# Hybrid decoder step on one core: rows of the norms' factors by transposing spread columns

## The chip, the cores and the metric

The kernel runs on one core of a Trainium2 chip. The metric is device time in microseconds, the median of several executions. TensorE appears in the profile as PE (matmuls) and PEld (its weight loads), VectorE as DVE, ScalarE as ACT, GpSimd as POOL, and the queue that issues the transfers as SP.

## What is computed

The reference is one inference step of one layer, for a prompt of 1024 tokens and for 8 sequences of 4 new tokens, 1056 tokens of width 1024 in all. Each sub-layer stands between two RMS norms:

```python
def rmsnorm(x, g):
    xf = x.astype(jnp.float32)
    y = xf * lax.rsqrt(jnp.mean(xf * xf, axis=-1, keepdims=True) + RMS_EPS)
    return (y * g.astype(jnp.float32)).astype(x.dtype)
...
    def half_ffn(x, j, gpre, gpost):
        y = swiglu(rmsnorm(x, g[gpre]), ffn_w_gate[l, j], ffn_w_up[l, j], ffn_w_down[l, j])
        return x + 0.5 * rmsnorm(y, g[gpost])

    x = half_ffn(x, 0, 0, 1)
    h = rmsnorm(x, g[2])
    ...
    u = jnp.concatenate([u_m, u_a], axis=-1)
    x = x + rmsnorm(u @ w_out[l], g[3])
    x = half_ffn(x, 1, 4, 5)
```

Between the two feed-forward halves, `h` is projected and passes through four mLSTM heads and eight heads of sliding-window attention. What matters here is the factor of a norm, `rsqrt(mean(x*x) + eps)`: one number per token.

## The kernel before

Activations are kept transposed: the 1024 features on partitions, in eight blocks of 128, and the tokens along the free axis. The 1056 tokens are cut into four quarters `q` of `QW` = 264 columns: 256 prompt tokens and 8 of the new ones. Two quarters form a half `g`.

There are three phases: the first feed-forward half, the mixer with `w_out`, the second feed-forward half. In each, products with weights (`pl`, `gu`, `pd`, `pz`, `pv`, `po`, `pw`) run over blocks of 128 outputs and all quarters. Each product is made of three matmuls in a reduced f32 format: weights and activations are split into a high and a low part by `split` (a cast on ACT, a subtraction on DVE), and `mm3` and its inlined copies multiply high by high, high by low and low by high. Weights come in through two buffers named `raw`.

A norm's factor is made as follows. The squares of the features are summed into a tile `acc`. `col_stats` sums over partitions by products with a column of ones and gives a PSUM tile `cs` with three columns: column `j` has, on its 128 partitions, the sums of the tokens that begin at `WIN[j]`, with `WIN = [0, 128, 136]`; so the third column repeats tokens 136 to 255 and adds the last eight. `rstd` turns them into factors by some ten small DVE operations on 128x3 elements. `row_bcast` makes a row of them again, 264 wide and repeated on all 128 partitions, in a PSUM tile `rb`: column `j` is read with its one element repeated 128 times along the free axis, as the stationary operand of a product with the identity. Two products are 128 columns wide, the third takes the last eight columns of the identity only. ACT then copies `rb` to SBUF, as `cr` in `post` (L443) or as `rrow` in `set_row` (L283). The tiles `cs`, `rb` and some others share a single PSUM buffer (tag `c`), so each is used only after the one ahead of it has been read.

`post` ends a sub-layer for one quarter: statistics, `row_bcast`, then y times `cr` plus the residual for four pairs of blocks (L448, L449) with the squares for the next norm, its statistics, and a second `row_bcast` into `rrow`. It runs for all four quarters of phases 1 and 2 with both rows, and for quarters 0 to 2 of phase 3 with `cr` alone: 11 calls of the first kind, 8 of the second. The last quarter of phase 3 is done by the class `Last`, in token layout with transposes, and makes no row. At the start, `load_x` loads tokens, computes the factors in token layout and makes the row of a quarter by two products with the identity and one with the eight new tokens' factors `xtr`.

The order of the work is written by a small planner, `Order`. Its clock `now` advances by a booked price with every product that `pe` issues: 4 x max(n, 64) / 2400 us for a plain f32 product of n columns, about 0.11 for a product of the reduced format and 0.11 for a transpose. After each group of three matmuls `tick` runs the side tasks (`load_x`, `post`, `blocks` and others) that have come due; each yields the time after which its next step is due, counted from the clock ahead of the step.

Of the kernel before, what the change touches and what calls it, by code (L numbers as in the profile page):

```python
# [16 lines left out]
P = 128  # L17
# [8 lines left out]


WIN = [0, 128, 136]
ROWP = [(0, 128, 0), (128, 128, 0), (256, 8, 120)]
STEPS = {1: [(0, 1), (2, 3)], 2: [(0, 1), (2, 3)], 3: [(0, 1), (2,), (3,)]}  # L30
NSLOT, NW, NRAW, NTMP = 66, 8, 2, 8
BANKS = dict(mm=3, a=2, b=2, c=1)
# [115 lines left out]
def pe(K, out, lhsT, rhs, start=True, stop=True, tr=False, **kw):  # L148
    n = int(np.prod(rhs.shape[1:]))
    if tr:  # L150
        K.nc.tensor.transpose(out, lhsT, rhs)  # L151
        K.od.now += 0.11
        return
    K.nc.tensor.matmul(out, lhsT, rhs, start=start, stop=stop, **kw)  # L154
    if rhs.dtype == F32R:
        K.od.now += 0.0025 + (n if n >= 213 else 256) / 2400
    else:
        K.od.now += (4 if rhs.dtype == F32 else 1) * max(n, 64) / 2400
# [7 lines left out]
def slot(K, name, dt=F32):  # L166
    return K.sp.tile([P, 2 * QW], dt, tag="s", name=nm(K, name))


def pair(t):  # L170
    return t.rearrange("p (a t) -> p a t", a=2)
# [10 lines left out]
def bank(K, name, tag="mm"):  # L182
    return K.pp[tag].tile([P, 512], F32, tag=tag, name=nm(K, name))


def sbank(K, name):
    return bank(K, name, "c")
# [64 lines left out]
def row_bcast(K, col):  # L252

    ps = sbank(K, "rb")
    for j, (a, w, b) in enumerate(ROWP):
        pe(K, ps[:, a:a + w], col[:, j:j + 1].to_broadcast([P, P]), K.ident[:, b:b + w])
    return ps[:, 0:QW]


# [20 lines left out]
def set_row(K, q, ps):  # L280

    row = K.cp.tile([P, QW], F32, tag=f"rrow{q}", name=nm(K, "rrow"), bufs=1)
    K.nc.scalar.copy(row, ps)  # L283
    K.r[q] = row


def stash(K, q, kp, x):

    t = K.dp.tile([P, 2 * QW], F32, tag=f"xs{q}{kp}", name=nm(K, "xs"))
    K.nc.sync.dma_start(t, x)  # L290
    K.xs[q][kp] = t


def load_tokens(K, src, w):

    t = [slot(K, "xt")[0:w, 0:512] for _ in range(2)]
    for i in range(2):
        K.nc.sync.dma_start(t[i], src[:, i * 512:(i + 1) * 512])
    return t


def token_norm(K, tt, both=False):

    nc = K.nc
    n = len(tt)
    ss = K.kp.tile([P, 6], F32, tag="xss", name=nm(K, "xss"), bufs=2)
    nc.vector.memset(ss, 1.0)
    for j, t in enumerate(tt):
        for i in range(2):
            w = t[i].shape[0]  # L310
            jk = tmp(K, "jk", 512)[0:w]
            o = ss[0:w, n * i + j:n * i + j + 1]
            if both and i == 0:
                nc.vector.tensor_tensor_reduce(out=jk, in0=t[i], in1=t[i], scale=1.0, scalar=0.0,
                                               op0=ALU.mult, op1=ALU.add, accum_out=o)
            else:
                nc.scalar.activation(jk, t[i], AF.Square, accum_out=o)
    s = small(K, "xsn", n)
    nc.vector.tensor_tensor(s, ss[:, 0:n], ss[:, n:2 * n], op=ALU.add)
    return rstd(K, s)  # L320


def load_sample(K):

    ps = bank(K, "xsT", "a")
    for k in range(KT):
        pe(K, ps[:, 32 * k:32 * k + 32], K.xt[k // 4][:, (k % 4) * P:(k % 4) * P + P], K.ident[0:32, 0:32], tr=True)
    K.xsT = slot(K, "xsT")[:, 0:256].rearrange("p (k t) -> p k t", k=KT)
    K.nc.vector.tensor_copy(K.xsT, ps[:, 0:256].rearrange("p (k t) -> p k t", k=KT))


def load_x(K, q):

    nc = K.nc
    tt = [load_tokens(K, K.A["x_prompt"][0, (2 * q + j) * P:(2 * q + j + 1) * P], P) for j in range(2)]
    if q == 0:
        K.xt = load_tokens(K, K.A["x_sample"].rearrange("b t d -> (b t) d"), 32)
    yield XW[0]
    with K.tc.high_priority():
        r = token_norm(K, tt + [K.xt] if q == 0 else tt, q == 0)  # L340
        if q == 0:
            K.xtr = K.cp.tile([32, 1], F32, tag="xtr", name="xtr")
            nc.vector.tensor_copy(K.xtr, r[0:32, 2:3])
    x = [slot(K, "xr") for _ in range(4)]
    for kp in range(4):

        ps = bank(K, "xT")
        for i in range(2):
            k = 2 * kp + i
            for j, t in enumerate(tt):  # L350
                pe(K, ps[:, (2 * i + j) * P:(2 * i + j + 1) * P], t[k // 4][:, (k % 4) * P:(k % 4) * P + P], K.ident,
                   tr=True)
        nc.scalar.copy(pair(x[kp])[:, :, 0:2 * P], ps.rearrange("p (a t) -> p a t", a=2))
        if q == 0 and kp == 0:
            load_sample(K)
        nc.gpsimd.tensor_copy(pair(x[kp])[:, :, 2 * P:QW], K.xsT[:, 2 * kp:2 * kp + 2, 8 * q:8 * q + 8])
        yield XW[1]
    while q and ("b", 0, q - 1, 3) not in K.od.done:
        yield 0.2
    with K.tc.high_priority():  # L360
        ps = sbank(K, "rb")
        for j in range(2):
            pe(K, ps[:, j * P:(j + 1) * P], r[:, j:j + 1].to_broadcast([P, P]), K.ident)
        pe(K, ps[:, 2 * P:QW], K.xtr.to_broadcast([32, P]), K.ident[0:32, 8 * q:8 * q + 8])
        set_row(K, q, ps[:, 0:QW])
    for kp in range(4):
        stash(K, q, kp, x[kp])
    yield XW[2]
    yield from blocks(K, 0, q, x, 0)
# [8 lines left out]
def blocks(K, phase, q, x, gpre):  # L378

    K.b[q], K.X[q] = [], []  # L380
    for kp in range(4):
        b = slot(K, "xb")
        for k in (2 * kp, 2 * kp + 1):
            s = slice((k % 2) * QW, (k % 2) * QW + QW)
            K.nc.vector.scalar_tensor_tensor(b[:, s], x[kp][:, s], K.gain[:, gpre * 8 + k:gpre * 8 + k + 1], K.r[q],
                                             op0=ALU.mult, op1=ALU.mult)
        K.b[q].append(b)
        K.X[q].append(xsplit(K, b))
        K.od.done.add(("b", phase, q, kp))
        yield NP[0]  # L390
# [38 lines left out]
def post(K, phase, q, y, acc, half, nxt, gpre=None):  # L429
# [11 lines left out]
    yield PW[1]  # L441
    cr = tmp(K, "cr", QW)
    nc.scalar.copy(cr, row_bcast(K, c))  # L443
    yield 0.5
    acc = None
# [30 lines left out]
    if nxt == "mix":  # L476
        rc = K.kp.tile([P, 3], F32, tag=f"rc{q}", name=nm(K, "rc"), bufs=1)
        nc.vector.tensor_copy(rc, r)
        K.rc[q] = rc
    set_row(K, q, row_bcast(K, r))  # L480
    K.od.done.add(("r", phase, q))
    if nxt == "ffn":
# [1277 lines left out]
def program(ctx, tc, A, O):  # L1760
    K = setup(ctx, tc, A, O)
    load_gains(K)
    K.od.units += [*ffn_units(K, 0), *mix_units(K), *ffn_units(K, 1)]
    K.od.ahead = AHEAD
    K.od.spawn(load_x(K, 0))
    K.od.need(("b", 0, 0, 1))
    K.od.fill()
    for q in range(1, NQ):
        K.od.spawn(load_x(K, q), XQ[q])
    ffn(K, 1, 0, 1, "mix", 2)  # L1770
    mix(K)
    ffn(K, 3, 1, 5, None)
    K.od.drain()
# [30 lines left out]
```

## Time and profile before

| | us |
|---|---|
| median of 3 runs | 2019.58 |
| lowest, highest | 2016.46, 2020.38 |
| the profiled execution | 2019.21 |
| its span, first to last instruction | 2017.4 |

The profile is that of one execution. Matmuls are pipelined: a record's duration is its latency, and what one costs in a stream is the distance between starts. Weight loads overlap with matmuls. A row of the timeline gives the start, the time from the first start to the last end, engine, line, operation, output and inputs, the tile's shapes and the number of records; a bracket tells the idle time ahead and what ended it. A row of the windows gives a stretch, its length, each engine's busy time with its number of instructions, the granted TensorE clock, the DMA engines' share and GB/s.

### The profile page before, as it was taken

To read this page: it belongs to the slowest core of one execution; us is meant where nothing else is said; L and a number is where in the kernel's file an instruction comes from. 1 tells how busy PE (TensorE), PEld (TensorE's weight loads), DVE (VectorE), ACT (ScalarE), POOL (GpSimd) and SP (SyncE) were. 2 spreads that over 40 slices of the span, in tenths; PEclk is the share of its full clock that TensorE was granted. 3 is DMA by queue.
4 is the path that set the end of the run, shared out by engine and by line. 5 is a ranking of instruction groups with operands and counts; after the bars stand their busy time and mean duration, and the time that the engine had idled before them with its cause. 6 is when DMAs were issued, how large, how long until landed. Compare 5 with 4: busy or idle time off the path is not lost.

```text
span 2017.4 us, 40347 instructions
## 1 busy us (share of the span) xinstructions
PE 1986.5 (98%) x16178; PEld 1942.6 (96%) x16178; DVE 1168.4 (58%) x2822; ACT 874.9 (43%) x2087; POOL 35.6 (2%) x166
## 2 busy tenths in 40 slices
PE   7999999999999999999999999999999999999997
PEld 7999999999999999987999999999999999999997
DVE  5855555557238436467556758785555556534764
ACT  6533333336336332346244655353333334533553
POOL 0000000000000001100101000000000000000000
PEclk9999999999999999999999999999999999999999
DMA  6122222226346343201214143322222223545773
GB/s 234 65 85 77 90 69 74 76 95 177 108 142 208 104 102 124 68 1 38 68 53 134 57 133 116 108 78 82 65 84 80 91 64 120 167 129 162 226 223 116
DMA packets 279690, 216.66 MB, mean 107 GB/s; under 512 B 21032, under 2 KB 252640, under 8 KB 279488
## 3 DMA queue, kind: packets, MB, share of 16 engines
q1 hardware_dynamic: 279504, 214.11, 35.0%
q8 instruction: 126, 2.06, 0.5%
q14 instruction: 60, 0.49, 0.1%
HBM read 172.39 MB, written 42.49 MB: 107 GB/s over the span
## 4 chain that ended last, share of the span: by engine, by line
PE 91%; DVE 3%; DMA 3%; ACT 2%; issue 1%; SPq 0%; DVEq 0%; ACTq 0%
PE gu L154 41%; PE pd L154 23%; PE pz L154 7%; PE pw L154 4%; PE pl L154 4%; PE pv L154 3%; PE po L154 2%; DMA raw<-ffn_w_down 2%; PE cs L154 1%; PE rb L154 1%; PE swo L154 1%; PE sws L154 1%; PE E L154 1%; ACT wh L196 1%; PE swp L151 1%
## 5 line engine op out<-in xcount | busy, mean ns | idle before, releaser
L154 PE MATMUL gu<-Xh,wh 128*128 128x264 f32 x2240 | 636.6, 284 | 0.0
L154 PE MATMUL gu<-Xl,wh 128*128 128x264 f32 x2240 | 636.0, 284 | 0.0
L154 PE MATMUL gu<-Xh,wl 128*128 128x264 f32 x2240 | 635.1, 284 | 0.0
L197 DVE TENSOR_TENSOR wl<-raw,wh 128x512 fp32r<-128x512 f32 x458 | 301.6, 670 | 384.3 <-ACT wh L196 376.5
L154 PE MATMUL pd<-hq,wh 128*128 128x264 f32 x2816 | 520.8, 286 | 0.1
L196 ACT CAST wh<-raw 128x512 fp32r<-128x512 f32 x458 | 270.1, 602 | 459.4 <-PE pd L154 193.2
L154 PEld LDWEIGHTS pd<-hq,wh 128*128 128x128 f32 x2816 | 437.8, 189 | 0.4 <-ACT yo L853 0.4
L154 PEld LDWEIGHTS gu<-Xh,wh 128*128 128x128 f32 x2240 | 421.1, 188 | 0.5 <-ACT sc L752 0.2
L154 PEld LDWEIGHTS gu<-Xh,wl 128*128 128x128 f32 x2240 | 421.6, 188 | 0.0
L154 PEld LDWEIGHTS gu<-Xl,wh 128*128 128x128 f32 x2240 | 421.3, 188 | 0.0
L154 PE MATMUL pd<-hq,wl 128*128 128x264 f32 x1408 | 401.1, 285 | 0.0
L154 PEld LDWEIGHTS pd<-hq,wl 128*128 128x128 f32 x1408 | 265.4, 188 | 0.2 <-DVE wl L197 0.2
L752 ACT COPY sc<-gu 128x264 f32<-128x264 f32 x240 | 91.0, 380 | 272.2 <-PE gu L154 268.0
L197 DVE TENSOR_TENSOR wl<-ws,wh 128x512 fp32r<-128x512 f32 x160 | 108.8, 690 | 87.6 <-ACT wh L196 84.7
L763 DVE TENSOR_TENSOR h<-gu,sc 128x264 f32<-128x264 f32 x120 | 51.8, 432 | 102.2 <-PE gu L154 83.3
L154 PE MATMUL pz<-xh,wh 128*128 128x264 f32 x352 | 102.3, 291 | 0.6 <-DVE z L1684 0.6
L154 PE MATMUL pz<-xh,wl 128*128 128x264 f32 x352 | 100.8, 286 | 0.0
L154 PE MATMUL pz<-xl,wh 128*128 128x264 f32 x352 | 100.5, 285 | 0.0
L196 ACT CAST wh<-ws 128x512 fp32r<-128x512 f32 x160 | 95.9, 623 | 4.1 <-PE pl L154 2.5
L764 ACT ACTIVATE h<-h 128x264 f32<-128x264 f32 x120 | 50.9, 425 | 106.5 <-DVE h L763 106.5
L769 DVE TENSOR_TENSOR sc<-gu,sc 128x264 f32<-128x264 f32 x120 | 51.6, 432 | 56.8 <-PE gu L154 51.4
L154 PE MATMUL pl<-Xh,wh 128*128 128x264 f32 x256 | 72.9, 299 | 3.3 <-ACT Xh L196 2.1
(368 smaller groups left out, 2969.6 us busy)
## 6 DMA issues: line engine op xcount, KB each, us to landing
raw<-ffn_w_down SPq DMA_DIRECT2D x80, 512.0 KB
raw<-ffn_w_gate SPq DMA_DIRECT2D x44, 512.0 KB
raw<-ffn_w_up SPq DMA_DIRECT2D x44, 512.0 KB
h<-h SPq DMA_DIRECT2D x80, 264.0 KB
hq<-h SPq DMA_DIRECT2D x160, 132.0 KB
raw<-ffn_w_down SPq DMA_DIRECT2D x40, 384.0 KB
x<-xs SPq DMA_DIRECT2D x48, 264.0 KB
raw<-w_in SPq DMA_DIRECT2D x21, 512.0 KB
```

Source lines behind the costliest of these rows:

```text
L151: K.nc.tensor.transpose(out, lhsT, rhs)
L154: K.nc.tensor.matmul(out, lhsT, rhs, start=start, stop=stop, **kw)
L196: K.nc.scalar.copy(hi, src)
L197: (eng or K.nc.vector).tensor_tensor(lo, src, hi.bitcast(F32), op=ALU.subtract)
L752: nc.scalar.copy(sc[n][:, g], ps)
L763: nc.vector.tensor_tensor(d, bk[tg, g], sc[n][:, g], op=ALU.add)
L764: nc.scalar.activation(d, d, AF.Silu)
L769: nc.vector.tensor_tensor(sc[n][:, g], src, sc[n][:, g], op=ALU.add)
```

## The change

`row_bcast` issues three transposes, each 128 columns wide, of the spread columns in place of the three products with (parts of) the identity. The third goes to columns 136 to 263 and is issued first, then the second to 128 to 255, then the first; columns 136 to 255 are thus written twice, with the same tokens' factors. `load_x` makes its two wide parts by transposes; the part of the new tokens stays a product. The table `ROWP` goes.

```diff
 WIN = [0, 128, 136]
-ROWP = [(0, 128, 0), (128, 128, 0), (256, 8, 120)]
...
 def row_bcast(K, col):
 
     ps = sbank(K, "rb")
-    for j, (a, w, b) in enumerate(ROWP):
-        pe(K, ps[:, a:a + w], col[:, j:j + 1].to_broadcast([P, P]), K.ident[:, b:b + w])
+    for j in (2, 1, 0):
+
+        pe(K, ps[:, WIN[j]:WIN[j] + P], col[:, j:j + 1].to_broadcast([P, P]), K.ident, tr=True)
     return ps[:, 0:QW]
...
         ps = sbank(K, "rb")
         for j in range(2):
-            pe(K, ps[:, j * P:(j + 1) * P], r[:, j:j + 1].to_broadcast([P, P]), K.ident)
+            pe(K, ps[:, j * P:(j + 1) * P], r[:, j:j + 1].to_broadcast([P, P]), K.ident, tr=True)
         pe(K, ps[:, 2 * P:QW], K.xtr.to_broadcast([32, P]), K.ident[0:32, 8 * q:8 * q + 8])
```

In `pe`, `tr=True` issues `transpose(out, lhsT, rhs)` and adds 0.11 to the planner's clock.

## The prediction

> **What bounds the kernel now.** I read the head of the page first, then the chain of work that ended last by engine, then the table of windows.
>
> ```profile
> span 2017.4 us, 40347 instructions
> PE 1986.5 (98%) x16178; PEld 1942.6 (96%) x16178; DVE 1168.4 (58%) x2822; ACT 874.9 (43%) x2087; POOL 35.6 (2%) x166
> PE 91%; DVE 3%; DMA 3%; ACT 2%; issue 1%; SPq 0%; DVEq 0%; ACTq 0%
> ```
>
> PE has something in flight during 98% of the span and makes up 91% of the chain, so a microsecond of PE time that disappears from a dense stretch is normally a microsecond of the end. The exceptions are stretches where PE waits for someone else; they come below. Where the touched work lies is read from the windows of 100 us, restricted to the tile `rb`:
>
> ```profile
> core 0: us, PE busy (x) PEld busy (x) ACT busy (x), PEclk, DMA share, GB/s
> 0.00:100.00 100.00, 4.60 (x24) 3.88 (x24) 1.52 (x4) 1.00 0.44 151
> ...
> 600.00:700.00 100.00, 3.40 (x24) 3.32 (x24) 1.54 (x4) 0.98 0.53 161
> 700.00:800.00 100.00, 3.05 (x24) 2.99 (x24) 1.52 (x4) 1.00 0.42 119
> ...
> 1200.00:1300.00 100.00, 5.99 (x48) 6.00 (x48) 2.73 (x8) 0.97 0.40 131
> ...
> 1800.00:1900.00 100.00, 1.56 (x12) 1.50 (x12) 0.76 (x2) 1.00 0.59 179
> 1900.00:2000.00 100.00, 0.73 (x6) 0.75 (x6) 0.37 (x1) 1.00 0.69 208
> ```
>
> The column after the time is PE's busy time with the number of records. All 138 `rb` records are here: 24 in the start (`load_x`, four times), 114 in 19 calls of `row_bcast` of six records each (4 + 4 + 8 + 2 + 1). Nothing else is touched.
>
> **The change part by part.** First the records of one product. The groups by line, shapes kept apart:
>
> ```profile
> L154 PE MATMUL rb<-ident,r 128*128 128x128 f32 x92 | 15.4, 292 | 2.8 <-DVE v L265 1.5 <-DVE r L276 1.3
> L154 PE MATMUL rb<-ident,r 128*128 128x8 f32 x38 | 5.6, 219 | 0.0
> L151 PE MATMUL yT<-ident,y 128*128 128x128 f32 x72 | 11.1, 277 | 3.4 <-DVE y L449 1.6 <-ACT y L556 1.0 <-ACT yo L853 0.7
> ```
>
> The code asks for 19 x 2 + 4 x 2 = 46 wide products and 19 narrow ones, and the trace has 92 and 38: an f32 product is two records, each with its own weight load. The f32 transposes `yT` are 24 calls in `Last` (12 in `first`, 12 in `second`) and 3 x 16 in `store_y`, 72 in all, and 72 records: one each. So `row_bcast` goes from six records to three and `load_x` loses two of its six. The means (292, 219, 277 ns) are latencies that overlap; the price has to be read from starts. The PE timeline around the last `row_bcast`, and around three transposes in the same kind of stream:
>
> ```profile
> 1939.14 0.28 PE L154 MATMUL pd<-hq,wl 128*128 128x264 f32 x1
> ...
> 1939.51 0.28 PE L154 MATMUL pd<-hq,wl 128*128 128x264 f32 x1
> 1939.62 0.73 PE L154 MATMUL rb<-ident,r 128*128 128x128 f32 x6
> 1940.21 0.49 PE L154 MATMUL pd<-hq,wh 128*128 128x264 f32 x2
> 1940.54 0.28 PE L154 MATMUL pd<-hq,wl 128*128 128x264 f32 x1
> ```
> ```profile
> 2001.11 0.28 PE L154 MATMUL pd<-hq,wl 128*128 128x264 f32 x1
> ...
> 2001.47 0.28 PE L154 MATMUL pd<-hq,wl 128*128 128x264 f32 x1
> 2001.60 0.49 PE L151 MATMUL yT<-ident,y 128*128 128x128 f32 x3
> 2001.84 0.49 PE L154 MATMUL pd<-hq,wh 128*128 128x264 f32 x2
> 2002.17 0.28 PE L154 MATMUL pd<-hq,wl 128*128 128x264 f32 x1
> ```
>
> Three `pd` matmuls take 1939.51 - 1939.14 = 0.37 us undisturbed. With six `rb` records between them they take 1940.54 - 1939.51 = 1.03, so the six cost 0.66 us (0.11 each). Three transposes: 2002.17 - 2001.47 = 0.70, less 0.36, costs 0.34. **Saved per call: 0.32 us.** The narrow product was already as dear per record as a wide one, so that the new third transpose computes 128 columns where 8 were needed costs nothing extra.
>
> No row of before shows a transpose whose stationary operand is one column repeated. Bounds: as cheap as `yT` (0.11), or as dear as the product it replaces (0.22, its two records). The product's weight load already reads the repeated column, at the pace of its neighbours, so I take 0.11 and keep 0.22, no gain at all, as the other end.
>
> Eighteen calls stand in streams like this one: 18 x 0.32 = 5.8 us. The one left runs at a lower granted clock:
>
> ```profile
> 632.81 1.16 PE L154 MATMUL rb<-ident,r 128*128 128x128 f32 x6 [1.55 <-DVE v L265]
> 633.82 0.57 PE L154 MATMUL pd<-hq,wh 128*128 128x264 f32 x1
> ```
>
> Six records take 1.01 us from start to start; half is 0.5. For `load_x`, the first call and the third:
>
> ```profile
> 13.11 1.23 PE L154 MATMUL rb<-ident,r 128*128 128x128 f32 x4 [1.08 <-DVE r L276]
> 14.26 0.59 PE L154 MATMUL rb<-ident,xtr 32*128 32x8 f32 x2
> ...
> 41.99 0.60 PE L154 MATMUL rb<-ident,r 128*128 128x128 f32 x4
> 42.53 0.38 PE L154 MATMUL rb<-ident,xtr 32*128 32x8 f32 x2
> ```
>
> The first spends 14.26 - 13.11 = 1.15 us on four records, so two fewer save 0.57; in a stream, 0.54 on four, so 0.27, three times 0.8. Gross: 5.8 + 0.5 + 0.57 + 0.8 = 7.7 us.
>
> What of it is hidden. In the start PE waits for loads, so I count half of the first call's 0.57. In two places another engine ends the wait behind the call. These windows have PE, PEld, DVE, ACT and POOL, then the granted clock:
>
> ```profile
> 1284.00:1288.00 4.00, 3.58 (x32) 3.40 (x30) 3.83 (x10) 1.50 (x3) 0.00 (x0) 1.00 0.35 136
> 1288.00:1292.00 4.00, 3.44 (x17) 3.13 (x17) 3.66 (x10) 0.79 (x2) 0.00 (x0) 0.56 0.18 70
> 1292.00:1296.00 4.00, 4.00 (x22) 4.00 (x22) 4.00 (x12) 1.27 (x2) 0.00 (x0) 0.58 0.00 0
> 1296.00:1300.00 4.00, 4.00 (x36) 4.00 (x35) 0.78 (x4) 0.07 (x1) 0.00 (x0) 1.00 0.02 4
> ...
> 1900.00:2000.00 100.00, 96.32 (x788) 94.68 (x786) 58.63 (x116) 53.82 (x119) 0.00 (x0) 1.00 0.69 208
> ```
>
> From 1284 to 1296 DVE is busy 11.5 of 12 us while PE starts only 71 matmuls, against 36 per 4 us behind it: the `rb` just ahead of it gains PE nothing. In the last 100 us PE idles 3.7 us and the chain runs through loads of `ffn_w_down`, so of the three calls of the third stage I count half. Discount: 0.3 + 0.32 + 0.5 = 1.1, and 0.2 for waits I can't place. **Net 6.4 us.**
>
> Two side effects. The planner that decides how far matmuls are issued between two pieces of side work books 0.53 us for a `row_bcast` now (0.213 + 0.213 + 0.107) and 0.33 afterwards, at 0.11 per transpose. In `post` the step behind `row_bcast` is due 0.5 us after its start: today it is due at once, afterwards only one round of three matmuls later (0.34 booked). So DVE's first multiplication of the residual path (L448) may stand a little later among its neighbours in 11 places. Nothing waits for that at once: the results are used whole stages later, except at 1284 to 1296. I cost it at 0, between -4 and +4 us, the size of one such stretch: at 36 per 4 us, 108 matmuls would have fitted into these 12 us; 37 are missing, at 4 / 36 us each 4.1 us, and a shift of order can remove or repeat it. Second, columns 136 to 255 are written twice, by the third part and then by the second; both come from PE in order, and `cs` sums already write one cell repeatedly at a record pace of 0.11, so 0.
>
> The profiled execution took 2019.21 us, its span 2017.4; 2019.21 - 6.4 = 2012.8. The median of the three runs is 0.4 above it: **2013.2 us**.
>
> **The rivals.** *Gain lost in waits*: PE reaches its waits for DVE and for `ffn_w_down` earlier and waits longer. For it: those windows, and 77.3 us in which ACT's casts wait for `ffn_w_down`:
>
> ```profile
> ACT wh L196 <- DMA raw<-ffn_w_down: 77.3, 44, 3.9
> PE rb L154 <- DVE v L265: 1.5, 1, 1.5
> ```
>
> Against it: the loads are released by buffers that PE's own progress frees, and PE's longest wait for a product outside the start is 1.5 us. If all of the second stage's eight calls (2.6) and the third's three (1.0) go, 2.8 us remain: 2016.8.
>
> *No cheaper transpose*: either 0.22 each with a repeated column, or the overlapping columns make a transpose wait for the one ahead of it to drain (277 ns against 110, twice per call, 0.33: the whole saving of a call). 2019.6. Against it: the rows above.
>
> *More stretches like 1284 to 1296* (the slower side): a `post` whose order shifts makes PE wait for DVE, the granted clock falls behind the wait, and each new stretch costs 4.1 us. It sits where `cs` and `rb` share their single PSUM buffer, as at 632.81, where `rb` waits 1.55 us until DVE has read `cs`. Two new ones eat the gain; from three on (12.3 - 6.4) the kernel is slower, about 2025.5. For it: both stretches of low clock (632 and 1288) lie at a `post`. Against it: 11 calls of `post` make only two now.
>
> *The clock gate starves on transposes*: PE slows down behind each `row_bcast`. A stretch at 0.56 to 0.58 costs (0.44 + 0.42) x 4 = 3.4 us by the windows above; four new ones give 2013.2 + 13.6 = 2026.8. Against it, a row of the PE timeline and the window around it, where transposes stand among matmuls:
>
> ```profile
> 1945.05 0.60 PE L151 MATMUL xT<-ident,x 128*128 128x128 f32 x4
> ...
> 1944.00:1948.00 4.00, 4.00 (x36) 4.00 (x36) 2.91 (x5) 1.71 (x4) 0.00 (x0) 1.00 0.55 157
> ```
>
> The clock stays at 1.00. No row shows transposes beside a wait. The Trainium skill ("TensorE: Matmul & The Clock Gate", "Part 4: PE-mode transpose") says that transposes do not count as busy for the clock in the way matmuls do, and so speaks against the change. By that rule the time would be this rival's; by the window of 1944 to 1948, which disagrees with it among dense matmuls, the sum stays as it is.
>
> **How the numbers follow.** Forecast 0.58 (own range 2010 to 2015.5); gain lost in waits 0.20 (2016.8); no cheaper 0.08 (2019.6); more stretches 0.10 (2025.5); clock gate 0.04 (2026.8). This kernel's measurement can tell about 0.2% from no change, 4.0 us: faster is below 2015.5, slower above 2023.6. Faster 0.58, same 0.28, slower 0.14. The range reaches from the forecast with one stretch of low clock gone (2013.2 - 4.1 = 2009) to the case without gain and its scatter, 2021.5; that leaves the two slow cases out, and a little below.
>
> **What would show it.** Right: 65 `rb` records of the transpose's line beside 8 of `xtr`, a `row_bcast` in a dense stream costing 0.34 us, the same stretches of low clock at the same places, and the third stage starting about 5 us earlier. Wrong: `rb` transposes more than 0.2 us apart (no cheaper); new windows with fewer than 30 matmuls per 4 us near 640 to 670, 750 to 800 or 1205 to 1300 (more stretches), or with the clock below 1 and no wait of PE ahead of it (clock gate); or PE's idle time in the last 130 us up by about what was saved earlier (lost in waits).

## The result: slower by 0.3%, and the profile after

The changed kernel took 2024.92 us (median of 6 runs, 2022.97 to 2026.56). The kernel before took 2016.26 us on the same chip (6 runs, 2013.94 to 2020.38). The ratio is 1.0032, 95% interval 1.002 to 1.0044: slower by some 6.5 us, where 6.4 us of gain were forecast, and outside the range. The profiled execution took 2023.34 us, its span is 4.2 us longer than before.

The head of the page after, and the chain of waits by engine:

```profile
span 2021.6 us, 40221 instructions
PE 1982.5 (98%) x16113; PEld 1937.8 (96%) x16113; DVE 1168.8 (58%) x2822; ACT 873.0 (43%) x2087; POOL 38.4 (2%) x166
PE 88%; DMA 4%; DVE 4%; ACT 2%; issue 1%; SPq 0%; DVEq 0%; ACTq 0%
```

PE has 65 records less and is busy 4.0 us less (1986.5 before), yet the span grew: PE's idle time went from 30.9 to 39.1 us, and in the chain DMA and DVE each gained a point of what PE lost. In the same chain by line, the loads of `ffn_w_down` went from 1.6% to 3.0% of the span. So the work became shorter, and the waits longer by more. The PE timeline around the last `row_bcast`, and the groups of the tile `rb`:

```profile
1941.36 0.29 PE L153 MATMUL pd<-hq,wl 128*128 128x264 f32 x1
...
1941.73 0.28 PE L153 MATMUL pd<-hq,wl 128*128 128x264 f32 x1
1941.85 0.49 PE L150 MATMUL rb<-ident,r 128*128 128x128 f32 x3
1942.09 0.49 PE L153 MATMUL pd<-hq,wh 128*128 128x264 f32 x2
1942.42 0.28 PE L153 MATMUL pd<-hq,wl 128*128 128x264 f32 x1
```
```profile
L150 PE MATMUL rb<-ident,r x65: 270/272/474, 12.0 to 1942.1; 128*128 128x128 f32 x65
L153 PE MATMUL rb<-ident,xtr x8: 251/271/377, 12.6 to 56.9; 32*128 32x8 f32 x8
```

Read as in the prediction: 1942.42 - 1941.73 = 0.69, less 0.37 for three undisturbed matmuls, is 0.32 us for three transposes (0.66 for the six records before). The transposes are as cheap as forecast. The windows of the last stage, columns as in the prediction's table of five engines:

```profile
1700.00:1800.00 100.00, 99.56 (x816) 99.13 (x814) 48.91 (x104) 45.82 (x112) 0.00 (x0) 1.00 0.46 134
1800.00:1900.00 100.00, 97.29 (x800) 96.50 (x799) 55.09 (x115) 43.89 (x99) 0.00 (x0) 1.00 0.58 173
1900.00:2000.00 100.00, 94.89 (x774) 92.65 (x772) 58.57 (x116) 53.53 (x119) 0.00 (x0) 1.00 0.72 218
```

Before, the same three windows had PE busy 100.00, 99.31 and 96.32 us. Here it idles 3.9 us more, with the clock at 1.00. Stage by stage, from the first and last starts of the tiles (us; stages are bounded by the first start of the tile named, the last ones by the last end):

```
                        before  after
start to first gu         78.7   81.0
gu, first run            408.7  410.8
pd                       266.6  264.1
pz                        66.0   65.5
pv                       200.5  200.7
po                       127.8  131.1
pw                       109.7  108.5
to the last pl            59.5   55.4
gu, second run           408.0  409.5
pd, the last stage       281.4  284.5
rest                      10.5   10.5
```

`pw` shows the gain alone: four calls of `row_bcast` stand there, 4 x 0.32 = 1.3, and it is 1.2 shorter. Several stages without a single changed instruction in them, the two runs of `gu` and `po`, are longer, and so is the last stage. Not all of that recurs: a second profile of the changed kernel (after_again, below) has 79.0 us to the first `gu` and 127.8 for `po` as before, but again 410.8 for the first run of `gu` and 286.0 for the last stage.

### The profile page after: what moved, and what is told of

Same layout as the page of the kernel before. It is cut to its first block, busy times and chain, and to the rows that moved or that the text cites. A ratio compares the mean times of both kernels' runs of the same rounds, so it can differ in the third digit from the quotient of the medians.

```text
span 2021.6 us, 40221 instructions
## 1 busy us (share of the span) xinstructions
PE 1982.5 (98%) x16113; PEld 1937.8 (96%) x16113; DVE 1168.8 (58%) x2822; ACT 873.0 (43%) x2087; POOL 38.4 (2%) x166
## 4 chain that ended last, share of the span: by engine, by line
PE 88%; DMA 4%; DVE 4%; ACT 2%; issue 1%; SPq 0%; DVEq 0%; ACTq 0%
PE gu L153 40%; PE pd L153 21%; PE pz L153 7%; PE pw L153 4%; PE pl L153 4%; PE pv L153 3%; DMA raw<-ffn_w_down 3%; PE po L153 2%; PE cs L153 1%; PE sws L153 1%; DVE wl L196 1%; PE swo L153 1%; ACT wh L195 1%; PE E L153 1%; DVE xb L385 1%
```

## The experiments

All ratios are to the kernel before, run in turn with the experiment on the same chip, with 95% intervals.

### Planner or transposes

The first suspicion was the planner's booking, since it changes the written order: laid side by side in the two traces, 349 of the 16040 records outside `rb` have another output or input at the same place. **t_oldbook** keeps the transposes and books them as the products were booked; **p_newbook** keeps the products and books them as the transposes are. The first diff is against the changed kernel, the second against the kernel before; `load_x` is booked likewise.

```diff
-        pe(K, ps[:, WIN[j]:WIN[j] + P], col[:, j:j + 1].to_broadcast([P, P]), K.ident, tr=True)
+        pe(K, ps[:, WIN[j]:WIN[j] + P], col[:, j:j + 1].to_broadcast([P, P]), K.ident, tr=True, book=4 * (64 if j == 2 else P) / 2400)
```
```diff
-        pe(K, ps[:, a:a + w], col[:, j:j + 1].to_broadcast([P, P]), K.ident[:, b:b + w])
+        pe(K, ps[:, a:a + w], col[:, j:j + 1].to_broadcast([P, P]), K.ident[:, b:b + w], book=0.11)
```

> The transposes of the change, but the planner's clock is advanced as for the products before (0.213, 0.213 and 0.107 us in row_bcast, 0.213 each in load_x), so that the written order of the side work stays that of before. Theory A (the order did it: the planner books 0.2 us less per row, side work moves, and that costs more than the transposes save): faster than before by 4 to 8 us, ratio 0.996 to 0.998. Theory B (transposes themselves cost something the timeline of before does not show, a clock that falls or a drain that is waited for): as slow as the changed kernel, ratio about 1.003.

> The products of before, but each wide or narrow product of row_bcast, and the two wide ones of load_x, advance the planner's clock by 0.11 us as the transposes do, so that the written order of the side work is that of the changed kernel. Theory A: slower than before by the cost of the order with nothing saved, 12 to 16 us, ratio 1.006 to 1.008. Theory B: as before, ratio 1.000 within 0.001.

> The changed kernel once more, for a second trace and on the same chip as its neighbours. Both theories: ratio 1.002 to 1.005.

> The kernel before once more, for a second trace. Both theories: the same stretches of waits and of low clock at 632 and 1288 us; the length of the dense stages (gu) shows how much of 408.7 against 410.8 us is scatter between executions.

Measured: t_oldbook 1.0019 (1.0009 to 1.003), p_newbook 1.0072 (1.006 to 1.0084), the changed kernel again 1.0037 (1.0023 to 1.0051); the kernel before in one run 2014.36 us, span 2012.5. With the order of before restored the transposes were still slower than the products, so the booking isn't the whole cause. The new order with products is the slowest of all; here the stretch that the prediction feared does open, at 1290 us, where the mixer ends and the third stage begins:

```profile
PE rb L154 <- DVE r L278: 6.7, 1, 6.7
```
```profile
1290.00:1294.00 4.00, 0.50 (x5) 0.41 (x4) 3.47 (x11) 1.16 (x2) 0.00 (x0) 0.91 0.18 68
1294.00:1298.00 4.00, 0.85 (x4) 0.88 (x5) 3.91 (x12) 1.41 (x3) 0.00 (x0) 0.50 0.41 153
1298.00:1302.00 4.00, 3.53 (x18) 3.44 (x18) 2.12 (x6) 1.01 (x2) 0.00 (x0) 0.50 0.13 50
1302.00:1306.00 4.00, 3.60 (x16) 3.30 (x16) 4.00 (x10) 0.63 (x1) 0.00 (x0) 0.50 0.01 2
```

The first row is p_newbook's wait of PE for DVE (total, times, longest), the others are its windows: PE starts 9 matmuls in 8 us, and runs at half clock from 1293 us on. In the profiled execution of the changed kernel the same place is harmless:

```profile
1284.00:1288.00 4.00, 4.00 (x35) 4.00 (x34) 3.99 (x12) 1.33 (x3) 0.00 (x0) 1.00 0.40 147
1288.00:1292.00 4.00, 2.13 (x19) 1.95 (x18) 3.77 (x10) 1.66 (x3) 0.00 (x0) 1.00 0.36 137
1292.00:1296.00 4.00, 4.00 (x35) 4.00 (x35) 3.99 (x11) 1.27 (x2) 0.00 (x0) 1.00 0.21 72
```

PE waits 1.87 us in the second of these windows, and the clock stays at 1.00. In after_again, the same program, the same wait of 1.87 us is followed by half clock:

```profile
1288.00:1292.00 4.00, 4.00 (x23) 4.00 (x22) 4.00 (x10) 1.06 (x2) 0.00 (x0) 0.61 0.02 4
```

Two observations remained from the stage table. The last stage took 284.5 to 286.0 us in every kernel with transposes and 279.7 to 281.4 with products, in either order; and the first run of `gu` took 410.5 or more in t_oldbook and in the new order, 408.7 to 409.0 in before.

### Parts of the change

Four kernels with transposes in some places only, all booked as the products were, so that nearly every instruction keeps its place: **x_3** in phase 3's three calls, **x_load** in `load_x`, **x_12** in phases 1 and 2, **x_rows** in all calls of `row_bcast`.

```diff
+    if phase in (3,):
+        for j in (2, 1, 0):
+            for i in range(1):
+                pe(K, ps[:, WIN[j]:WIN[j] + P], col[:, j:j + 1].to_broadcast([P, P]), K.ident, tr=True,
+                   book=4 * (64 if j == 2 else P) / 2400 / 1)
+    else:
+        for j, (a, w, b) in enumerate(ROWP):
...
```

The condition reads `(1, 2)` in x_12 and `(1, 2, 3)` in x_rows. x_load has the change's lines in `load_x`, with the booking:

```diff
-            pe(K, ps[:, j * P:(j + 1) * P], r[:, j:j + 1].to_broadcast([P, P]), K.ident)
+            pe(K, ps[:, j * P:(j + 1) * P], r[:, j:j + 1].to_broadcast([P, P]), K.ident, tr=True, book=4 * P / 2400)
```

> Transposes in the three calls of row_bcast in phase 3 alone, booked by the planner as the products were; nothing else differs from the kernel before, so the first 1,700 us should agree with it in every theory. Theory A (the head start is lost and more in the last stage, which waits for the weights of ffn_w_down): the last stage, from the end of gu's second run to the end of pd's, takes 284 to 286 us in place of 280 to 281, and the whole is about 4 us slower, ratio near 1.002. Theory B (the last stage lost time only because all that came before it was moved): it takes 279 to 281 us and the whole is 0 to 1 us faster, ratio 0.9995 to 1.000.

> Transposes in load_x alone, booked as the products were; row_bcast keeps its products. The tiles of X stand where they stood in the transposes-with-the-old-booking run, with one pair of slots exchanged. Theory A (the pace of the dense product gu depends on where its moving operands stand): gu's first run takes 410 to 411 us in place of 408.7 to 409.0, its matmuls come 0.5 to 0.6 ns later each from the first exchanged tile on, and the whole is 1 to 2 us slower, ratio 1.0005 to 1.001. Theory B (the pace has another cause): 408.7 to 409.0 us, and the whole is 0.5 us faster, ratio 0.9997.

> Transposes in the calls of row_bcast in phases 1 and 2 alone, booked as the products were; phase 3 and load_x keep their products. Theory A (the transposes save what was forecast, 0.32 us a call, wherever the stage waits for no weights, and the loss has other causes that this kernel leaves out): gu's first run 408.7 to 409.0 us, pw 108.3 in place of 109.7, the last stage 280 to 281 us, the whole 3 to 5 us faster, ratio 0.9975 to 0.9985. Theory B (the gain of the transposes is lost in waits anywhere): ratio 0.9995 or more.

> Transposes in all calls of row_bcast, booked as the products were; load_x keeps its products. Theory A (as in the two runs with parts of it): gu's first run 408.7 to 409.0 us, the last stage 284 to 286 us, the whole within 1 us of the kernel before, ratio 0.9995 to 1.0005. Theory B (the parts don't add up, the last stage depends on when it starts): the last stage 279 to 281 us and the whole 4 to 5 us faster, ratio 0.9975.

Measured: x_3 1.0025 (1.0015 to 1.0035), x_load 1.0039 (1.0025 to 1.0053), x_12 1.0048 (1.003 to 1.0067), x_rows 1.0032 (1.0019 to 1.0044). All four are slower, and the last stage took 285.5 to 286.4 us in all, also in x_load and x_12, which have nothing but products there. So x_3 came out with the numbers of its theory A (286.0 us, about 1.7 of them by a half-clock window at 1937 us; 1.0025) and for another reason than that theory gave: transposes *in* the last stage don't cost it time. What stands apart from the last stage came as expected: `gu`'s first run 410.5 us in x_load, 408.7 in x_12 and 409.0 in x_rows, `pw` 108.5 in the two with transposes there. But x_load as a whole was 8 us slower in place of 1 to 2, and x_12 10 us slower in place of 3 to 5 faster. Of x_12's loss a part is the clock: the mean granted clock of its timed runs was 0.9932, that of the kernel before 0.9963, and 0.0031 of 2018 us are 6 us.

What the four share was found by laying x_load beside the kernel before: in the last stage ACT, DVE and SP have the same instructions in the same order, PE's matmuls agree within 0.1 us with the second profile of before for the first 160 us, and then ACT's casts start later and later because weights land later. So the loads were measured one by one, from the issue on SP to the end of the last packet in the trace, over ten mostly undisturbed 512 KB loads early in the last stage (the 10th to the 24th load, without the smaller ones). Median: 3.12 us in before, 3.77 in the changed kernel, 3.74 in x_3. One of these loads in x_3: its issue in SP's timeline, and the windows from 2.0 to 3.8 us behind it; the last two columns are the DMA engines' share and GB/s:

```profile
1770.38 0.37 SPq L221 DMA_DIRECT2D raw<-ffn_w_down  x1
```
```profile
1772.38:1773.38 1.00, 1.00 (x10) 1.00 (x10) 0.31 (x1) 0.74 (x2) 0.00 (x0) 1.00 1.06 320
1773.38:1773.58 0.20, 0.20 (x4) 0.20 (x3) 0.20 (x1) 0.20 (x1) 0.00 (x0) 1.00 0.50 149
1773.58:1773.88 0.30, 0.30 (x5) 0.30 (x4) 0.18 (x1) 0.30 (x2) 0.00 (x0) 1.00 0.20 60
1773.88:1774.18 0.30, 0.30 (x5) 0.30 (x4) 0.00 (x0) 0.30 (x2) 0.00 (x0) 1.00 0.03 9
```

Until 3.0 us after the issue the load runs as it does in the quick kernels; then it has a tail at a small part of the rate, to 3.7 us. With it every step of the loop load, cast, subtract, free the buffer, next load is 0.6 us longer. In x_3 this is so already in the first `pd` stage, from some 490 us on (median of the 512 KB loads there 3.80 us, before 3.17), 1,370 us before its first transpose. No execution of a transpose can be the cause. What differs at that time is only what is fixed before the start, and the obvious difference was the length of TensorE's program: a transpose is one record where a product is two.

### The length of TensorE's program

**x_3d** issues each of x_3's nine transposes twice (`range(2)`, and half the price each), which gives the old number of records. **after_end33** is the changed kernel with 33 one-column products behind the last work, read by nobody, and **x_rows_end29** is x_rows with 29. **before_in4k** has an unread input of 4 KB more and the instructions of before.

```diff
     K.od.drain()
+    ps = sbank(K, "rb")
+    for i in range(33):
+        pe(K, ps[0:32, i:i + 1], K.ident[0:32, 0:32], K.ident[0:32, i % 32:i % 32 + 1])
```
```diff
     arrays, A, O = {}, {}, {}
+    arrays["aa_pad"] = np.zeros(1024, np.float32)
```

> As the run with transposes in phase 3 alone, but each of its nine transposes is issued twice, so that TensorE's program is as long as that of the kernel before (16178 matmul records). In the run with single ones every load of ffn_w_down took 3.7 to 3.8 us from issue to landing in place of 3.1, from 490 us on, long before the first transposes at 1861 us. Theory A (the length of the program decides where the weights come to lie in device memory, and that sets the loads' time): 3.1 us a load, the last stage 280 to 281.5 us, ratio 0.9995 to 1.0005. Theory B (it is something that transposes bring with them, however long the program): 3.7 to 3.8 us, 285 to 286 us, ratio 1.002 to 1.003.

> The changed kernel with 33 one-column f32 products that nobody reads behind its last work, which make TensorE's program about as long as before (two matmul records each, 66 in place of the 65 saved). Theory A (length of the program): loads of ffn_w_down 3.1 us, the last stage 279 to 281 us, the whole 4 to 6 us faster than the changed kernel, ratio to before 0.999 to 1.0015. Theory B (transposes themselves, or the new order): 3.7 to 3.8 us, 284 to 286 us, ratio 1.003 or more.

> Transposes in all calls of row_bcast, booked as the products were, products in load_x, and 29 one-column products behind the last work that bring TensorE's program back to its length (58 records in place of the 57 saved). Theory A (length): loads 3.1 us, gu's first run 408.7 to 409.0 us, the last stage 279 to 280.5 us, the whole 4 to 6 us faster than the kernel before, ratio 0.997 to 0.998. Theory B: 3.7 to 3.8 us, 285 to 286 us, ratio 1.002 to 1.003.

> The kernel before, with one more input of 4 KB, given ahead of all others and read by nobody; every instruction is that of the kernel before. Theory A (where the weights lie in device memory sets the loads' time, and a small shift can change it): loads of ffn_w_down 3.7 to 3.8 us and the last stage 284 to 286 us, ratio 1.002; or, where the shift is not one that matters, 3.1 us as before. Theory C (only the instructions matter): 3.1 us, ratio 1.000. So 3.7 us would show that it is the place; 3.1 us would leave it open.

Measured: x_3d 1.0003 (0.9994 to 1.0012), after_end33 1.0006 (0.9989 to 1.0022), x_rows_end29 0.9986 (0.9972 to 1.0), before_in4k 0.9993 (0.9985 to 1.0002). In all four a load took 3.07 to 3.16 us and the last stage 278.1 to 282.5. Adding idle work at the end made the changed kernel 0.3% faster: 1.0037 to 1.0006 is 6.3 us. Its last stage, to be compared with the windows of after above:

```profile
1700.00:1800.00 100.00, 99.89 (x818) 99.46 (x818) 48.17 (x103) 44.88 (x108) 0.00 (x0) 1.00 0.47 139
1800.00:1900.00 100.00, 100.00 (x827) 99.39 (x826) 57.92 (x120) 46.37 (x103) 0.00 (x0) 1.00 0.62 187
1900.00:2000.00 100.00, 96.83 (x792) 95.21 (x791) 55.95 (x113) 52.61 (x117) 0.00 (x0) 1.00 0.67 200
```

PE idles 3.3 us in these 300 us, in the changed kernel 8.3. The extra input changed nothing, which leaves open whether the place of the weights has to do with it.

x_rows_end29 is faster than the kernel before by 2.8 us in the median of the ratio, with an interval that ends at no gain. It stayed short of the 4 to 6 us expected. One place where it loses shows in its profiled execution, which took 2020.38 us:

```profile
1100.00:1105.00 5.00, 2.99 (x31) 1.84 (x28) 2.11 (x8) 0.00 (x0) 0.33 (x3) 0.81 1.04 298
1105.00:1110.00 5.00, 5.00 (x29) 4.14 (x28) 2.27 (x6) 3.14 (x4) 0.37 (x2) 0.50 0.44 127
1110.00:1115.00 5.00, 5.00 (x33) 4.15 (x30) 2.35 (x8) 0.69 (x1) 0.37 (x2) 0.50 0.59 171
```

Ahead of it PE waits for the load of the mLSTM state, 2.0 us there and 0.6 in before (the table of waits of the same stretch: total, times, longest):

```profile
PE sinter L154 <- DMA Cb<-state_mlstm_C: 2.0, 2, 1.3
```

Then four clock windows at 0.5 follow one another, 13.65 us in all, which cost half of that, 6.8 us. In the profile of the kernel before this stretch stands at 1.00. Over the timed runs the difference is smaller: the mean clock was 0.9942, that of the kernel before 0.9954, which makes 2.4 us.

### What is left of the gain, and does a longer program hurt

**e1_end33** is t_oldbook with 33 such products, **x_13_end17** has transposes in phases 1 and 3 only and 17 products, **before_end16** is the kernel before with 16, so 32 matmul records longer. The edits are those shown already.

> Transposes everywhere as in the change, booked as the products were, and 33 one-column products behind the last work. Theory A (the planner's new order costs the rest): gu's first run 410.5 us as without the fill-up, the last stage 278 to 280 us, the whole 1 to 3 us faster than the kernel before, ratio 0.9985 to 0.9995, between x_rows_end29 (0.9986) and after_end33 (1.0006). Theory B (the transposes in load_x and the place of the tiles of X cost the rest, and the order nothing): as after_end33, 1.0000 to 1.0010.

> Transposes in row_bcast in phases 1 and 3, products in phase 2 and in load_x, old bookings, 17 one-column products behind the last work (34 matmul records in place of the 33 saved). Theory A (phase 2's transposes bring half-clock windows near 1100 us that take their gain back): no such window from 1095 to 1115 us in its profile, the stretch from the first po to the first pw 127.6 to 128 us, the whole 3 to 5 us faster than the kernel before, ratio 0.9975 to 0.9985. Theory B (those windows fall by chance): ratio 0.9985 to 0.9992, the share of its calls (11 of 19) in the gain of x_rows_end29.

> The kernel before with 16 one-column products that nobody reads behind its last work: TensorE's program is 32 matmul records and 32 weight loads longer, and nothing else differs. Theory A (any change of the length can move the weights): loads of ffn_w_down 3.7 us and the last stage 285 us, ratio 1.002 to 1.003. Theory B (only a length below that of before does): 3.1 us, 280 to 281 us, ratio 0.9995 to 1.0005.

Measured: e1_end33 0.9997 (0.9983 to 1.001), x_13_end17 1.0003 (0.9992 to 1.0013), before_end16 0.9996 (0.9985 to 1.0007); loads 3.06 to 3.09 us in all. A longer program costs nothing that shows here. x_13_end17's last stage took 283.2 us though its loads were quick, so the loads don't fix that stage's length alone. x_13_end17 missed both of its theories: it has no transposes in phase 2, and its profile still has a half-clock window at 1101.7 us and 130.0 us for the stretch from `po` to `pw`. So these windows aren't bound to phase 2's transposes. e1_end33, x_rows_end29 and after_end33 can't be told apart within their intervals, so neither the planner's new order nor `load_x` could be given a price of its own here.

### A step, and whose length

**x_3_end2** and **x_3_end4** are x_3 with 2 and 4 such products. **x_3_pool18** is x_3 with 18 more instructions on GpSimd, as many as TensorE lacks (nine matmul records and nine weight loads).

```diff
     K.od.drain()
+    t = small(K, "spare", 8)
+    for i in range(18):
+        K.nc.gpsimd.memset(t, 0.0)
```

> Transposes in phase 3 alone, with 2 one-column products behind the last work, four matmul records and four weight loads: TensorE's program has 10 instructions less than before, where x_3 without them has 18 less. Theory A (a step at a length): loads 3.7 us or 3.1 us and nothing between. Theory B (the loads' time goes with the length gradually): about 3.4 us.

> The same with 4 products: 2 instructions less than before. Theory A (a step): 3.7 or 3.1 us; 3.1 us here with 3.7 us for the run with 2 would place the step in between. Theory B (gradual): about 3.15 us.

> Transposes in phase 3 alone, with 18 memsets of one small tile on GpSimd behind the last work: the programs of all engines together are as long as before, TensorE's is 18 instructions shorter. Theory A (the sum of all programs counts): loads 3.1 us, the last stage 280 to 282 us. Theory B (TensorE's program alone counts): 3.7 us, 285 to 286 us.

One run each, beside 2018.05 us of the kernel before: 2016.17, 2015.69 and 2027.39 us; loads 3.09, 3.09 and 3.71 us. It is a step, not a slope, and the length of GpSimd's program doesn't count. The load of x_3 shown above, in x_3_end2 (windows at the same distances from the issue):

```profile
1767.26 0.37 SPq L221 DMA_DIRECT2D raw<-ffn_w_down  x1
```
```profile
1769.26:1770.26 1.00, 1.00 (x10) 1.00 (x10) 0.31 (x1) 0.74 (x2) 0.00 (x0) 1.00 1.06 320
1770.26:1770.46 0.20, 0.20 (x4) 0.20 (x3) 0.20 (x1) 0.20 (x1) 0.00 (x0) 1.00 0.06 15
1770.46:1770.76 0.30, 0.30 (x5) 0.30 (x4) 0.18 (x1) 0.30 (x2) 0.00 (x0) 1.00 0.00 0
```

The tail is gone, with two unread products more at the end of a program of 16169 matmul records:

```profile
PE 1983.8 (98%) x16173; PEld 1939.4 (96%) x16173; DVE 1168.0 (58%) x2822; ACT 873.7 (43%) x2087; POOL 35.6 (2%) x166
```

All traced kernels in order of that number (load: median as above; last stage: last `gu` to last `pd`; x_3_pool18's last stage holds two half-clock windows):

```
                 records  load us  last stage us   ratio
after              16113   3.77        284.5       1.0032
after_again        16113   3.71        286.0       1.0037
t_oldbook          16113   3.77        284.5       1.0019
x_rows             16121   3.73        286.4       1.0032
x_12               16130   3.72        286.0       1.0048
x_3                16169   3.74        286.0       1.0025
x_3_pool18         16169   3.71        289.4       one run
x_load             16170   3.69        285.5       1.0039
x_3_end2           16173   3.09        281.5       one run
x_3_end4           16177   3.09        280.8       one run
before             16178   3.12        281.4       1
before_again       16178   3.10        279.7       one run
p_newbook          16178   3.13        279.9       1.0072
x_3d               16178   3.07        282.5       1.0003
before_in4k        16178   3.16        280.8       0.9993
after_end33        16179   3.09        279.0       1.0006
x_rows_end29       16179   3.10        278.1       0.9986
e1_end33           16179   3.08        279.9       0.9997
x_13_end17         16179   3.09        283.2       1.0003
before_end16       16210   3.06        280.7       0.9996
```

The step lies between 16170 and 16173 records; all eight traces below it have the slow loads, all twelve above it the quick ones, whatever their order, their transposes and the chip they ran on. By which path TensorE's program reaches the loads is not shown. That the program's length moves something else in device memory, the weights or the lists of the transfers, is a guess; no run here could see an address there. One hint lies in the traces: they also record the fetching of the programs, packets of 16 KB on the queue `q8 instruction`. All eight traces with slow loads hold 126 of them; of the twelve others seven hold a 127th, in the last 9 us of the span or just behind it. A step at the length where one more such block is needed would fit, but the two traces of the kernel before differ in this count too (126 and 127), so it is not shown.

## Why the prediction was wrong

**Right: the change itself.** One record per transpose (65 and 8), 0.32 us for three, so 0.34 saved per call where 0.32 was taken; the overlapping columns cost nothing; `pw` 1.2 us shorter with four calls. "No cheaper transpose" fell. "The clock gate starves on transposes" found no support: the changed kernel's windows from 1284 to 1296, which hold a `row_bcast` and the wait behind it, stand at 1.00 in one profile and fall to half clock in the other, and the kernel before, with products, has half clock at the same place (0.56 and 0.58 in the prediction's windows). Ahead of the end the two profiles of the changed kernel and that of after_end33 have 3, 3 and 2 half-clock windows, the two of the kernel before 3 and 2. The rule cited there (the Trainium skill, "TensorE: Matmul & The Clock Gate", "Part 4: PE-mode transpose": transposes don't count as busy for the clock in the way matmuls do) isn't seen in these traces, and three transposes among matmuls can't refute it either.

**The step that failed: "Nothing else is touched."** With it the sum held every load and every other matmul at its price of before. Each of these moved.

- *The loads.* Removing 65 records from TensorE's program took it below a length at which the 512 KB loads of `ffn_w_down` go from 3.1 to 3.7 us. In the first `pd` stage, whose loads are slow too, that costs little or nothing: x_3, with the same instructions there as before, takes 265.4 us, x_3_end2 with quick loads 265.6, the two profiles of the kernel before 264.4 and 266.6 (the latter with a half-clock window at 633 us). In the last stage it does, since there the casts wait for the loads. Price: four pairs that differ by the filled-up length alone (x_3 and x_3d, after_again and after_end33, x_rows and x_rows_end29, t_oldbook and e1_end33) differ by 0.0022, 0.0031, 0.0046 and 0.0022, which is 4.4 to 9.3 us, 6.1 in the mean. x_3 and x_3d differ by doubled transposes, the others by products at the end.
- *The pace of `gu`.* The side effect of the planner was costed at 0 between -4 and +4, as a matter of waits. In the profile it shows up otherwise: in the dense first run of `gu`, where nothing waits, matmuls come a little later each. The windows from 100 to 480 us for that tile, in before, the changed kernel and x_load:

```profile
100.00:480.00 380.00, 379.76 (x3128) 379.55 (x3127) 55.23 (x128) 49.53 (x130) 1.00 0.28 87
```
```profile
100.00:480.00 380.00, 379.76 (x3110) 379.55 (x3109) 55.67 (x130) 48.99 (x129) 1.00 0.27 83
```
```profile
100.00:480.00 380.00, 379.76 (x3113) 379.55 (x3112) 55.15 (x128) 49.56 (x130) 1.00 0.28 86
```

18 matmuls fewer in 380 us: 122.2 ns each in place of 121.5, over 3360 of them 2.3 us, and the stage is 2.1 longer. The second run keeps its pace: 2965 records in the 360 us from 1340 on in both kernels. That its row in the stage table is 1.5 longer is mostly a matter of the bounds, since before issues seven of its 3360 matmuls (0.9 us) ahead of the last `pl` and the changed kernel none; some 0.5 us are waits. In the first run x_3, x_12, x_rows, x_3d and those filled up from them have 121.4 to 121.5, and x_load, t_oldbook, e1_end33, p_newbook and the changed kernel 122.0 to 122.2. x_load's expectation put this down to the place of `gu`'s moving operands, the tiles of `X`. That fits, but no kernel moved the tiles alone and the traces hold no addresses, so it is not shown.
- *Half-clock windows.* The prediction took the stretches of low clock as fixed. In the traces the clock falls to 0.5 for 3.41 us or a multiple of it, ahead of the end in all cases but one (x_load at 979 us) behind 3.4 us in which PE sat idle for 0.4 to 2.8 us, and not behind every such stretch. Each window costs 1.7 us, half its length; the profiles have one to seven of them before the end, and they stand at other places from kernel to kernel. The Trainium skill ("TensorE: Matmul & The Clock Gate", "What's actually happening") describes a free-running window of 3413 ns; the trace agrees with 3.413 us.

**The remainder.** With the loads back to 3.1 us the changed kernel (after_end33) still has a ratio of 1.0006 (0.9989 to 1.0022), 1.2 us slower than before, where 6.4 us of gain were forecast. Of these 7.6 us the pace of `gu` explains 2.1, and the mean clock of the timed runs (0.9947 against 0.9954) by estimate 1.4; some 4 us, with an uncertainty of about 3, stay open. A single profile can't settle it: the span of after_end33 is 2014.3 us, those of the kernel before are 2017.4 and 2012.5.

**The rivals.** "Gain lost in waits" named the right place, and the sign set down for it came: PE's idle time from 1800 to 2000 rose from 4.4 to 7.8 us. But it let the waits eat at most what had been saved, 2016.8, because it took the loads' own time as given. The forecast's own sign, a third stage that starts 5 us earlier, did not come: the last `pl`, behind which `gu` runs alone, starts at 1317.1 us where it was 1317.5. "More stretches like 1284 to 1296" happened in p_newbook, with the new order and products (a wait of 6.7 us), not in the changed kernel; of the places that the prediction named, after_end33 has one half-clock window, at 788.8 us.

## What to carry to other kernels

When a kernel changes by a few tenths of a per cent, compare the stages that the edit doesn't touch first, down to the time of a single load, before explaining the ones that it does. An edit that shortens one engine's program can shift the speed of a tensor's transfers, ahead of the edit too: restore the length with idle instructions at the end, and see whether the difference goes. Here that turned 1.0037 into 1.0006, and the variant with transposes in `row_bcast` alone, the old bookings and the fill-up was the best at 0.9986, not clearly ahead of the kernel before.

## What the runs showed of the hardware

- Loads of 512 KB in one tensor took 3.1 or 3.7 us, by a step at a length of TensorE's program between 16170 and 16173 matmul records, and the difference was a tail in which 9 to 150 GB/s flowed after the bulk at 320. Loads of 512 KB of `ffn_w_up`, `ffn_w_gate` and `w_in` did not show it: their medians are 3.3 to 3.5 us in the kernels of both kinds.
- The Trainium skill ("DMA: Bandwidth & Descriptors", "Latency and other measured facts") reports copies between tensors in device memory that slow down at row pitches of 2 MiB and more, and calls their mechanism an inference. `ffn_w_down` has a row pitch of 4 KB, so that row does not cover this case, and no run here shows whether the cause is related.
- The pitch of dense matmuls in the first run of `gu` was 121.4 to 121.5 or 122.0 to 122.2 ns, and the same in both profiles of the kernel before and in both of the changed kernel; in the second run it was 121.5 to 121.6 ns in all twenty traces.
- The clock fell to 0.5 behind waits shorter than the 3.41 us or more for which it then stayed there: 0.42 us of idle PE from 1284 to 1288 in the kernel before, a wait of 1.87 us in after_again. The same 1.87 us in the changed kernel's first profile had no such effect.
